# The first MLP product of one layer by Strassen's seven products, on an fp32 kernel of two transformer layers

## The chip, the cores and the metric

The kernel runs on one core of a Trainium2 chip. The metric is device time in microseconds (us): the median of the runs of one program. A profile is one more execution of the same program, in which every instruction is recorded.

The engines are TensorE (PE in the rows; its weight loads are a row of their own, PEld), VectorE (DVE), ScalarE (ACT), GpSimd (POOL) and SyncE (SP, which starts most transfers). Each engine works through its own instructions in program order; an instruction whose inputs are not there, or whose output buffer is still in use, holds up all that stand behind it on its engine. TensorE writes into PSUM, eight banks per core, the other engines into SBUF.

## The reference, cut to what matters

```python
def squared_relu_mlp(h, w1, w2):
    return jnp.square(jax.nn.relu(h @ w1)) @ w2

for layer in range(2):
    mod_x = silu(c) @ ada_w[layer] + ada_b[layer]      # six vectors of 1024; mod_c likewise for the context
    hx = modulate(rmsnorm(x, norm1_g[layer]), sh1, sc1)
    mx, mc = hybrid_mixer(hx, hc, w_in[layer], ...)    # retention and gated linear attention, 4 heads each
    x = x + g1 * (mx @ w_out[layer])
    hx = modulate(rmsnorm(x, norm2_g[layer]), sh2, sc2)
    x = x + g2 * squared_relu_mlp(hx, w_mlp1[layer], w_mlp2[layer])
    # the same for the 256 context tokens, in the first layer only
return rmsnorm(x, final_g)
```

There are 512 latent and 256 context tokens, 1024 features, 4096 hidden features, all in fp32. What is changed is `h @ w1` of the first layer, 768 tokens x 1024 x 4096.

## The kernel before, in words

Activations lie with features on the partitions: eight tiles of 128 features x 768 tokens. A product in fp32 is made from three products of a shorter type, float32r: each operand is split into a high part (a cast, `hi`, on ScalarE) and a low part (the rest, `lo`, a subtraction), and `mm3` (L437 to L439) issues high by high, high by low and low by high. A k tile (128 of the summed features) of an output tile thus takes three matmuls over 512 tokens and three over 256.

Weights come as slabs of 128 x 1024 (512 KB). `Slab.split` makes the two parts, the cast on ScalarE (L244) and the subtraction on VectorE (L245), into a ring of `NSPL` = 6 slots. `run` goes through a list of items in order; before and behind each item `advance` emits the splits of the slabs that come next, as far as the ring allows: a slab may take a slot when the last item that uses that slot's slab has been emitted.

The MLP of layer 1 (`l == 0`) runs in 8 blocks of 512 hidden features. Four `m1` items per block make the hidden features: each ends in a chain (`m1_chain`, L1207 to L1212) of ReLU and square on ScalarE, the exact square on GpSimd and the low part `hidl` on VectorE. `m2` items then multiply them by the second weight, and `residual` (L535, VectorE) adds each finished PSUM bank into `x`. Seven PSUM banks rotate under all these products (an eighth is kept for small ones), so that an eighth product must wait until the first one's bank has been read. The `m2` items of block u stand between the `m1` items of block u + 1. A chain's next step is emitted when the next item ticks (`Chains.tick`), so the order on every engine is the order in which the items emit.

In the same stretch `ada_sums` works out layer 2's six modulation vectors: 96 VectorE instructions of 128 x 1024 multiply `ada_w` by the condition and add (L340, L342), one pair per small `ada` item.

Of the kernel before, what the change touches and what calls it, by code (L numbers as in the profile page):

```python
# [9 lines left out]
F32 = mybir.dt.float32  # L10
# [6 lines left out]
P = 128  # L17
D = 1024
# [11 lines left out]
UFF = 512  # L30
UT = UFF // P
NU = FF // UFF
WCOL = 1024
NSLOT = 36
NSPL = 6
NRAW = 4
AHEAD = 4


class Item:  # L40
    """A piece of the program: emits instructions; may need weight slabs; a stage runs one block after its deps."""
# [54 lines left out]
class Act:  # L96
    """A moving operand in two float32r parts, made by chains for token ranges."""
# [10 lines left out]
# one block of projections and the attention stages that run behind it, per line; at most NSLOT tiles live  # L108
# [30 lines left out]
def build(ctx: ExitStack, tc, a):  # L139
# [44 lines left out]
    # ---- constants and inputs  # L184
# [32 lines left out]
    # silu(c) of both vectors, as 32 stationary columns (30 of them zero) per k tile  # L217
# [100 lines left out]
    # the second layer's: weighted sums over the k tiles on the vector engine, one product to add the partitions  # L318
# [5 lines left out]
    def ada_sums(l):  # L324
        acc = tp.tile([P, 2, WCOL], F32, tag="rtab", name=f"adaacc_{l}")
        todo = [(u, kk) for u in range(6) for kk in range(KK)]

        def load(i):
            u, kk = todo[i]
            w = wraw.tile([P, WCOL], F32, tag="raw", name=f"adaw_{l}_{u}_{kk}")  # L330
            nc.sync.dma_start(w, a["ada_w"][l, kk * P : (kk + 1) * P, u * WCOL : (u + 1) * WCOL])
            return w

        nxt = load(0)
        for i, (u, kk) in enumerate(todo):
            w, nxt = nxt, load(i + 1) if i + 1 < len(todo) else None
            for v in range(2):
                c = cs[:, kk, v : v + 1]
                if kk == 0:
                    nc.vector.tensor_scalar(acc[:, v], w, c, None, op0=ALU.mult)  # L340
                else:
                    nc.vector.scalar_tensor_tensor(acc[:, v], w, c, acc[:, v], op0=ALU.mult, op1=ALU.add)  # L342
            yield
            if kk == KK - 1:
                pt = psa.tile([P, 512], F32, tag="psa", name=f"ada_{l}_{u}")
                for v in range(2):
                    for c in range(4):
# [1087 lines left out]
```

## Time and profile before

| what | us |
|---|---|
| runs, median (lowest, highest) | 1659.98 (1659.19, 1660.61) |
| span of the profiled execution | 1658.9 |
| TensorE busy | 1618.7 |
| VectorE busy | 946.9 |
| ScalarE busy | 629.5 |
| GpSimd busy | 201.6 |

The profiled execution's span runs from the first instruction to the last and lies 1.1 us below the median of the runs; a time worked out from the trace is carried to the runs by adding that. Busy times are sums over instructions, and overlapping ones on TensorE are counted once.

### The profile page before, as it was taken

To read this page: it belongs to the slowest core of one execution; us is meant where nothing else is said; L and a number is where in the kernel's file an instruction comes from. 1 tells how busy PE (TensorE), PEld (TensorE's weight loads), DVE (VectorE), ACT (ScalarE), POOL (GpSimd) and SP (SyncE) were. 2 spreads that over 40 slices of the span, in tenths; PEclk is the share of its full clock that TensorE was granted. 3 is DMA by queue.
4 is the path that set the end of the run, shared out by engine and by line. 5 is a ranking of instruction groups with operands and counts; after the bars stand their busy time and mean duration, and the time that the engine had idled before them with its cause. 6 is when DMAs were issued, how large, how long until landed. Compare 5 with 4: busy or idle time off the path is not lost. (4 is left out here: it accounts for less than half of the span.)

```text
span 1658.9 us, 22890 instructions
## 1 busy us (share of the span) xinstructions
PE 1618.7 (98%) x9236; PEld 1384.2 (83%) x9236; DVE 946.9 (57%) x1491; ACT 629.5 (38%) x1083; POOL 201.6 (12%) x215
## 2 busy tenths in 40 slices
PE   5999999999999999999999999999999899999997
PEld 3778888888998888888888887888889888888887
DVE  5676664554755555555556476588466633443445
ACT  5535424562532222222212246363464532222232
POOL 3200021110111010110101121001110211010010
PEclk9999999999999999999999999999999999999999
DMA  9533433122323333333333222121123323223321
GB/s 323 175 127 126 137 108 102 39 88 90 103 89 127 115 127 109 120 102 116 126 115 127 95 88 66 51 77 52 51 89 128 103 89 102 91 100 102 102 64 51
DMA packets 57610, 173.80 MB, mean 105 GB/s; under 512 B 6208, under 2 KB 17792, under 8 KB 57504
## 3 DMA queue, kind: packets, MB, share of 16 engines
q1 hardware_dynamic: 55232, 164.85, 30.2%
q0 software_dynamic: 2272, 7.50, 1.2%
q8 instruction: 72, 1.18, 0.3%
q14 instruction: 34, 0.28, 0.0%
HBM read 168.13 MB, written 4.19 MB: 104 GB/s over the span
## 5 line engine op out<-in xcount | busy, mean ns | idle before, releaser
L437 PE MATMUL pm<-yh,hi_m 128*128 128x512 f32 (+1 forms) x800 | 279.6, 349 | 0.0
L437 PE MATMUL pm<-hidh,hi_m 128*128 128x512 f32 (+1 forms) x800 | 279.1, 349 | 0.0
L438 PE MATMUL pm<-yl,hi_m 128*128 128x512 f32 (+1 forms) x800 | 278.6, 348 | 0.0
L438 PE MATMUL pm<-hidl,hi_m 128*128 128x512 f32 (+1 forms) x800 | 278.4, 348 | 0.0
L439 PE MATMUL pm<-yh,lo_m 128*128 128x512 f32 (+1 forms) x800 | 278.2, 348 | 0.0
L439 PE MATMUL pm<-hidh,lo_m 128*128 128x512 f32 (+1 forms) x800 | 277.2, 347 | 0.0
L1208 ACT ACTIVATE relu<-pm 128x512 f32<-128x512 f32 (+1 forms) x100 | 51.1, 511 | 497.6 <-PE pm L439 493.9
L1212 DVE TENSOR_TENSOR hidl<-relu,hidh 128x512 fp32r<-128x512 f32 (+1 forms) x100 | 60.5, 607 | 296.0 <-POOL relu L1210 296.0
L1210 POOL TENSOR_TENSOR relu<-relu 128x512 f32<-128x512 f32 (+1 forms) x100 | 89.2, 893 | 760.3 <-ACT hidh L1209 760.2
L535 DVE SCALAR_TENSOR_TENSOR x<-pm,mod,x 128x512 f32<-128x512 f32 (+1 forms) x200 | 117.6, 640 | 106.6 <-PE pm L439 106.6
L437 PEld LDWEIGHTS pm<-yh,hi_m 128*128 128x128 f32 x800 | 152.6, 191 | 20.2 <-issue 1.2
L437 PEld LDWEIGHTS pm<-hidh,hi_m 128*128 128x128 f32 x800 | 151.5, 189 | 21.3 <-issue 1.1
L438 PEld LDWEIGHTS pm<-yl,hi_m 128*128 128x128 f32 x800 | 152.5, 191 | 18.8
L439 PEld LDWEIGHTS pm<-yh,lo_m 128*128 128x128 f32 x800 | 152.4, 191 | 19.0
L439 PEld LDWEIGHTS pm<-hidh,lo_m 128*128 128x128 f32 x800 | 151.1, 189 | 19.6
L438 PEld LDWEIGHTS pm<-hidl,hi_m 128*128 128x128 f32 x800 | 151.4, 189 | 18.9 <-issue 0.2
L245 DVE TENSOR_TENSOR lo_m<-raw_m,hi_m 128x1024 fp32r<-128x1024 f32 x126 | 154.0, 1222 | 10.6 <-ACT hi_m L244 10.6
L244 ACT CAST hi_m<-raw_m 128x1024 fp32r<-128x1024 f32 x128 | 129.6, 1040 | 51.6 <-DMA raw_m<-in_w_mlp 31.0
L342 DVE SCALAR_TENSOR_TENSOR adaacc<-adaw,cs,adaacc 128x1024 f32<-128x1024 f32 x84 | 103.9, 1278 | 0.0
L245 DVE TENSOR_TENSOR lo_wi<-raw_wi,hi_wi 128x1024 fp32r<-128x1024 f32 x49 | 60.6, 1249 | 29.8 <-ACT hi_wi L244 29.8
L437 PE MATMUL pwo<-yh,hi_wo 128*128 128x256 f32 (+1 forms) x224 | 70.9, 316 | 0.1
L438 PE MATMUL pwo<-yl,hi_wo 128*128 128x256 f32 (+1 forms) x224 | 70.3, 314 | 0.3 <-DVE yl L1056 0.3
(304 smaller groups left out, 2951.5 us busy)
## 6 DMA issues: line engine op xcount, KB each, us to landing
raw_m<-in_w_mlp SPq DMA_DIRECT2D x128, 512.0 KB, 3.5
adaw<-in_ada_w SPq DMA_DIRECT2D x80, 512.0 KB, 3.9
raw_wi<-in_w_in SPq DMA_DIRECT2D x58, 512.0 KB, 4.3
adaw<-in_ada_w SPq DMA_DIRECT2D x32, 256.0 KB, 6.3
raw_wo<-in_w_out SPq DMA_DIRECT2D x16, 512.0 KB, 3.4
x<-in_xT POOLq DMA_DIRECT2D x8, 384.0 KB, 7.8
x<-in_xT SPq DMA_DIRECT2D x8, 256.0 KB, 4.9
raw_wob<-in_w_out SPq DMA_DIRECT2D x4, 512.0 KB, 4.3
```

Source lines behind the costliest of these rows:

```text
L244: nc.scalar.copy(self.hi, self.raw)
L245: self.engine.tensor_sub(self.lo, self.raw, f32(self.hi))
L342: nc.vector.scalar_tensor_tensor(acc[:, v], w, c, acc[:, v], op0=ALU.mult, op1=ALU.add)
L437: nc.tensor.matmul(out, wh, xh, start=first, stop=False)
L438: nc.tensor.matmul(out, wh, xl, start=False, stop=False)
L439: nc.tensor.matmul(out, wl, xh, start=False, stop=last)
L535: nc.vector.scalar_tensor_tensor(xs[kk][:, t0:t1], pt[:, 0 : t1 - t0], mod[l][:, v, gate + kk : gate + kk + 1], xs[kk][:, t0:t1], op0=ALU. ...
L1208: nc.scalar.activation(r, pt[:, 0 : t1 - t0], AF.Relu)
L1210: nc.gpsimd.tensor_mul(r, r, r)
L1212: nc.vector.tensor_sub(a_.lo[:, t0:t1], r, f32(a_.hi[:, t0:t1]))
```

## The change: what it does

**The first MLP product of layer 1.** Layer 1's MLP now has 16 blocks u of 256 hidden features (`UTS` = (2, 4)); layer 2 keeps 512. Blocks 0 and 1 are computed as before. Blocks 2 to 15 take the Strassen-Winograd form: the weight of the block is cut in 2 x 2 (two output tiles by two halves of the 1024 features), the activations in 2 x 2 (two halves of the features by two halves of 384 tokens), and seven products of 384 tokens over 4 k tiles take the place of eight. That is 7 x 4 x 3 = 84 matmuls of 384 columns per block where 2 x 8 x 3 = 48 of 512 and 48 of 256 stood.

**Sums around it.** Four sums of weight quarters per block (`Pair.parts`: `s3`, `s1` in place in `a21`, `s2`, `s4`) are made on GpSimd, their casts on ScalarE and their low parts on VectorE. The sums of activations (`right_front`, `right_back`) are made once, during blocks 0 and 1. VectorE adds the products up (`u2`, `u3`, `c22`, `c21`, `c12`).

**What moves beside it.** The ring of split slabs has 5 slots (a `Pair` takes three and a small buffer of its own, `wsum`). Each `m2` item now covers two output tiles (`batch=2`), and layer 1 has twice as many, since a block has half the k tiles. `ada_sums` takes 64 steps of 768 columns, and the sums of the second condition are made as a product on ScalarE and an addition on GpSimd. The rotary and decay tables leave their own pool for the `work` slots (36 to 46 of them).

```diff
-NSPL = 6
+UTS = (2, 4)
+NSPL = 5
...
+    class Pair:
+        size, raws, held = 3, 2, 0
...
+        def split(self):
+            self.chain = ch.start(self.parts())
+
+        def parts(self):
+            h = WCOL // 2
+            (a11, a12), (a21, a22) = [(t[:, 0:h], t[:, h:WCOL]) for t in self.raw]
+            s2, s3, s4 = [temp(f"s{i}_{self.name}") for i in (2, 3, 4)]
+            nc.gpsimd.tensor_sub(s3, a11, a21)
+            nc.gpsimd.tensor_add(a21, a21, a22)
...
+            split(self.raw[0], hi[0], lo[0])
+            yield
+            nc.gpsimd.tensor_sub(s2, a21, a11)
+            nc.gpsimd.tensor_sub(s4, a12, s2)
+            two()
+            split(self.raw[1], hi[1], lo[1])
+            self.held = 0
+            yield
+            two()
+            split(s3, hi[2][:, 0:h], lo[2][:, 0:h])
+            split(s2, hi[2][:, h:WCOL], lo[2][:, h:WCOL])
+            yield
...
+            split(s4, hi[3], lo[3])
...
     def ada_sums(l):
...
-            for v in range(2):
-                c = cs[:, kk, v : v + 1]
...
-                    nc.vector.scalar_tensor_tensor(acc[:, v], w, c, acc[:, v], op0=ALU.mult, op1=ALU.add)
...
+                nc.vector.scalar_tensor_tensor(acc[0], w, c0, acc[0], op0=ALU.mult, op1=ALU.add)
+                nc.scalar.mul(w, w, c1)
+                nc.gpsimd.tensor_add(acc[1], acc[1], w)
...
+        def right_front(k):
...
+            for w, kk in ((t, k), (u, k + KH)):
+                nc.gpsimd.tensor_add(w, f32(norm2.out[kk].hi[:, 0:NT]), f32(norm2.out[kk].lo[:, 0:NT]))
+            yield
+            nc.gpsimd.tensor_sub(t[:, 0:H], t[:, H:NT], t[:, 0:H])
+            nc.vector.tensor_sub(t[:, H:NT], u[:, H:NT], t[:, H:NT])
+            yield
+            nc.gpsimd.tensor_sub(u[:, H:NT], u[:, H:NT], t[:, 0:H])
+            nc.gpsimd.tensor_sub(u[:, 0:H], u[:, 0:H], u[:, H:NT])
...
+        def product(pair, nm, x, pt, first=True):
+            ch.finish(pair.chain)
+            hi, lo, c0 = pair.part[nm]
+            for k in range(KH):
+                w = slice(c0 + k * P, c0 + k * P + P)
+                xh, xl = right[x, k]
+                for i, (wt, xt) in enumerate(((hi, xh), (hi, xl), (lo, xh))):
+                    nc.tensor.matmul(
+                        pt[:, 0:H], wt[:, w], xt, start=first and k == 0 and i == 0, stop=k == KH - 1 and i == 2,
+                        skip_group_check=True,
+                    )
+            ch.tick()
...
+            def p1():
+                product(pair, "a11", "b11", open_(1))
...
+            def p6():
+                product(pair, "s2", "t2", open_(2))
+                out(2, "u2", st["p1"])
+
+            def p7():
+                product(pair, "s3", "t3", open_(3))
+                out(3, "u3", st["u2"])
+
+            def p5():
+                product(pair, "s1", "t1", open_(4))
+                tail(out(4, "c22", st["u3"]), 1, H)
+
+            def p2():
+                product(pair, "a12", "b21", p[1], False)
...
+            def p4():
+                product(pair, "a22", "t4", p[3], False)
+                tail(out(3, "c21", st["u2"]), 1, 0)
+
+            def p3():
+                product(pair, "s4", "b22", p[4], False)
+                tail(out(4, "c12", st["u2"]), 0, H)
...
+            for u in range(2):
+                for i, q in enumerate(quarters):
+                    m2_item(u, [q], ada=False, batch=2)
...
+            strassen_items(2)
+            for u in range(2, NU - 1):
+                strassen_items(u + 1)
+                for q in quarters:
+                    m2_item(u, [q], batch=2)
```

**VectorE where an `m2` begins.** Before, around the first `m2` items of block 3 of 512 features (`lo_m1`, `lo_m2` are splits of slabs, `x0_0` the first output tile's residual, `adaacc` the modulation sums):

```order
L342 SCALAR_TENSOR_TENSOR adaacc_1_4292<-adaw_1_2_5_5841,cs_139,adaacc_1_4292 128x1024 x2
L245 TENSOR_TENSOR lo_m2_0_3_2_5920<-raw_m2_0_3_2_5845,hi_m2_0_3_2_5919 128x1024
L535 SCALAR_TENSOR_TENSOR x0_0_3342<-pm2_0_3_0_0_5923,mod0_149,x0_0_3342 128x512
L535 SCALAR_TENSOR_TENSOR x0_0_3342<-pm2_0_3_0_512_5924,mod0_149,x0_0_3342 128x256
L535 SCALAR_TENSOR_TENSOR x0_1_3344<-pm2_0_3_1_0_5925,mod0_149,x0_1_3344 128x512
L535 SCALAR_TENSOR_TENSOR x0_1_3344<-pm2_0_3_1_512_5926,mod0_149,x0_1_3344 128x256
L342 SCALAR_TENSOR_TENSOR adaacc_1_4292<-adaw_1_2_6_5913,cs_139,adaacc_1_4292 128x1024 x2
L245 TENSOR_TENSOR lo_m2_0_3_3_5986<-raw_m2_0_3_3_5917,hi_m2_0_3_3_5985 128x1024
L1212 TENSOR_TENSOR hidl_0_16_5990<-relu_0_16_0_6016,hidh_0_16_5989 128x512
L1212 TENSOR_TENSOR hidl_0_16_5990<-relu_0_16_512_6046,hidh_0_16_5989 128x256
L342 SCALAR_TENSOR_TENSOR adaacc_1_4292<-adaw_1_2_7_5979,cs_139,adaacc_1_4292 128x1024 x2
L245 TENSOR_TENSOR lo_m1_0_18_6058<-raw_m1_0_18_5983,hi_m1_0_18_6057 128x1024
```

Here one split stands between a step and the next residual.

VectorE now, around the beginning of `m2` of block 6 of 256 (whose hidden features are 12 and 13), behind the Strassen products of block 7 (hidden 14 and 15); the name `m1s_0_8` is the pair of block 8, rows with L1424 are `out`, L515 is `split`, L616 is `residual`:

```order
L1424 TENSOR_TENSOR c21_0_7_6210<-pst3_0_7_6138,u2_0_7_6131 128x384
L397 SCALAR_TENSOR_TENSOR adaacc_1_0_4626<-adaw_1_3_6_6176,cs_139,adaacc_1_0_4626 128x768
L1406 TENSOR_TENSOR hidl_0_15_6169<-c21_0_7_6210,hidh_0_15_6168 128x384
L1424 TENSOR_TENSOR c12_0_7_6233<-pst4_0_7_6153,u2_0_7_6131 128x384
L515 TENSOR_TENSOR lo0_m1s_0_8_6246<-raw_m1s_0_8_0_6090,hi0_m1s_0_8_6245 128x1024
L1406 TENSOR_TENSOR hidl_0_14_6194<-c12_0_7_6233,hidh_0_14_6193 128x384
L515 TENSOR_TENSOR lo1_m1s_0_8_6258<-raw_m1s_0_8_1_6092,hi1_m1s_0_8_6257 128x1024
L515 TENSOR_TENSOR lo2_m1s_0_8_6265<-s3_m1s_0_8_6241,hi2_m1s_0_8_6264 128x512
L515 TENSOR_TENSOR lo2_m1s_0_8_6265<-s2_m1s_0_8_6240,hi2_m1s_0_8_6264 128x512
L515 TENSOR_TENSOR lo3_m1s_0_8_6274<-s4_m1s_0_8_6242,hi3_m1s_0_8_6273 128x512
L616 SCALAR_TENSOR_TENSOR x0_0_3347<-pm2_0_6_0_0_6249,mod0_149,x0_0_3347 128x512
L616 SCALAR_TENSOR_TENSOR x0_0_3347<-pm2_0_6_0_512_6250,mod0_149,x0_0_3347 128x256
```

All five low parts of the pair of block 8 now stand ahead of the first residual of `m2` of block 6. The same order stands at the beginning of `m2` of blocks 2 to 13, each time with the pair two blocks on.

**GpSimd at the same place**, where before only the squares of the hidden features stood (L1404 is the square, L274 to L286 the sums of the pair):

```order
L1404 TENSOR_TENSOR c11_0_7_6191<-c11_0_7_6191 128x384
L1404 TENSOR_TENSOR c21_0_7_6210<-c21_0_7_6210 128x384
L399 TENSOR_TENSOR adaacc_1_1_4627<-adaacc_1_1_4627,adaw_1_3_6_6176 128x768
L1404 TENSOR_TENSOR c12_0_7_6233<-c12_0_7_6233 128x384
L274 TENSOR_TENSOR s3_m1s_0_8_6241<-raw_m1s_0_8_0_6090,raw_m1s_0_8_1_6092 128x512
L275 TENSOR_TENSOR raw_m1s_0_8_1_6092<-raw_m1s_0_8_1_6092 128x512
L285 TENSOR_TENSOR s2_m1s_0_8_6240<-raw_m1s_0_8_1_6092,raw_m1s_0_8_0_6090 128x512
L286 TENSOR_TENSOR s4_m1s_0_8_6242<-raw_m1s_0_8_0_6090,s2_m1s_0_8_6240 128x512
L399 TENSOR_TENSOR adaacc_1_1_4627<-adaacc_1_1_4627,adaw_1_3_7_6218 128x768
```

The four sums of a pair stand behind the squares of `c21` and `c12`, the last two results of the products.

**ScalarE where layer 1's projections turn from `vg` to `vr`** (the last of the copies of `vg` banks and what stands behind it), before:

```order
L763 COPY vg_0_3_706<-ps_vg0_5_962 128x128
L244 CAST hi_wi0_11_993<-raw_wi0_11_697 128x1024
L244 CAST hi_wi0_12_999<-raw_wi0_12_991 128x1024
L825 ACTIVATE gest_0_1_1011<-gst_0_1_919 128x18
L830 ACTIVATE gl_0_1_832<-gt_0_1_831,c_sgn_99 128x768
```

and now:

```order
L848 COPY vg_0_3_705<-ps_vg0_5_961 128x128
L248 CAST hi_wi0_10_992<-raw_wi0_10_696 128x1024
L248 CAST hi_wi0_11_998<-raw_wi0_11_990 128x1024
L248 CAST hi_wi0_12_1004<-raw_wi0_12_996 128x1024
L910 ACTIVATE gest_0_1_1016<-gst_0_1_918 128x18
```

Slab 10, which `vr` begins with, is cast behind the copies now, where its cast stood ahead of all of them before; layer 2 has the same order.

## Rows read from the trace of the kernel before

**Rows 1.** The page: busy time of each engine.

```profile
PE 1618.7 (98%) x9236; PEld 1384.2 (83%) x9236; DVE 946.9 (57%) x1491; ACT 629.5 (38%) x1083; POOL 201.6 (12%) x215
```

**Rows 2.** Windows: a stretch in layer 1's MLP (busy, granted clock).

```profile
core 0: us, PE busy (x) PEld busy (x) DVE busy (x) ACT busy (x) POOL busy (x), PEclk, DMA share, GB/s
470.00:970.00 500.00, 500.00 (x2909) 436.62 (x2908) 279.46 (x362) 120.06 (x185) 51.30 (x65) 1.00 0.36 116
```

**Rows 3.** Waits of TensorE, whole span: first and last of eleven rows.

```profile
PE ada L382 <- DMA adaw<-in_ada_w: 11.8, 1, 11.8
...
PE ps_d L452 <- DVE hl_n L521: 0.3, 1, 0.3
```

**Rows 4.** Timeline of TensorE in layer 1's MLP: start, duration, instruction.

```profile
599.12 0.39 PE L438 MATMUL pm<-yl,hi_m 128*128 128x512 f32 x1
...
601.61 0.28 PE L437 MATMUL pm<-yh,hi_m 128*128 128x256 f32 x1
...
602.45 0.28 PE L438 MATMUL pm<-yl,hi_m 128*128 128x256 f32 x1
```

**Rows 5.** Groups of VectorE by shape: count, busy us, mean ns, idle before.

```profile
L245 DVE TENSOR_TENSOR lo_m<-raw_m,hi_m 128x1024 fp32r<-128x1024 f32 x126 | 154.0, 1222 | 10.6 <-ACT hi_m L244 10.6
L342 DVE SCALAR_TENSOR_TENSOR adaacc<-adaw,cs,adaacc 128x1024 f32<-128x1024 f32 x84 | 103.9, 1278 | 0.0
L535 DVE SCALAR_TENSOR_TENSOR x<-pm,mod,x 128x512 f32<-128x512 f32 x120 | 87.6, 749 | 102.5 <-PE pm L439 102.5
...
L1212 DVE TENSOR_TENSOR hidl<-relu,hidh 128x512 fp32r<-128x512 f32 x60 | 42.5, 708 | 248.6 <-POOL relu L1210 248.6
L535 DVE SCALAR_TENSOR_TENSOR x<-pm,mod,x 128x256 f32<-128x256 f32 x80 | 37.0, 475 | 4.0 <-PE pm L439 4.0
...
L1212 DVE TENSOR_TENSOR hidl<-relu,hidh 128x256 fp32r<-128x256 f32 x40 | 18.1, 456 | 47.4 <-POOL relu L1210 47.4
```

**Rows 6.** Groups of ScalarE, shapes apart.

```profile
L244 ACT CAST hi_m<-raw_m 128x1024 fp32r<-128x1024 f32 x128 | 129.6, 1040 | 51.6 <-DMA raw_m<-in_w_mlp 31.0 <-PE pm L438 20.4 <-DVE hidl L1212 0.2
...
L1209 ACT ACTIVATE hidh<-relu 128x512 fp32r<-128x512 f32 x60 | 37.9, 632 | 1.9
L1208 ACT ACTIVATE relu<-pm 128x512 f32<-128x512 f32 x60 | 35.9, 598 | 442.8 <-PE pm L439 442.8
...
L1208 ACT ACTIVATE relu<-pm 128x256 f32<-128x256 f32 x40 | 15.3, 382 | 54.7 <-PE pm L439 51.0 <-DVE hidl L1212 3.7
```

**Rows 7.** Groups of GpSimd, shapes apart.

```profile
L1210 POOL TENSOR_TENSOR relu<-relu 128x512 f32<-128x512 f32 x60 | 63.6, 1060 | 699.9 <-ACT hidh L1209 699.8
L1210 POOL TENSOR_TENSOR relu<-relu 128x256 f32<-128x256 f32 x40 | 25.6, 642 | 60.4 <-ACT hidh L1209 60.4
...
L946 POOL TENSOR_TENSOR rq<-rq,rw_q 128x512 f32<-128x512 f32 x8 | 10.3, 1286 | 137.3 <-DVE rw_q L945 136.9
...
L983 POOL TENSOR_TENSOR rq<-rq,rtab 128x768 f32<-128x768 f32 x4 | 8.0, 1996 | 1.2 <-PE prs L966 1.0
```

**Rows 8.** Timeline of GpSimd and VectorE around 422 us, before layer 1's MLP.

```profile
422.09 1.29 POOL L510 TENSOR_TENSOR xn_n<-x,ssum_n 128x512 f32<-128x512 f32 x1 [3.31 <-DVE yl L521]
...
422.43 2.04 DVE L245 TENSOR_TENSOR lo_wob<-raw_wob,hi_wob 128x1024 fp32r<-128x1024 f32 x1 [0.47 <-ACT hi_wob L244]
```

**Rows 9.** Timeline of TensorE at its longest wait inside layer 2.

```profile
1297.16 0.80 PE L490 MATMUL st_n<-ssum_n,ones_d 128*128 128x256 f32 x1 [4.43 <-DVE ssum_n L473]
```

**Rows 10.** Windows behind that wait; columns as in Rows 2.

```profile
1297.00:1300.00 3.00, 2.84 (x11) 2.66 (x12) 2.62 (x4) 0.89 (x2) 1.16 (x2) 0.50 0.67 195
1300.00:1304.00 4.00, 4.00 (x26) 4.00 (x26) 3.57 (x8) 2.65 (x6) 1.03 (x2) 0.66 0.32 118
```

**Rows 11.** Timeline of ScalarE and VectorE where layer 2 turns from vg to vr.

```profile
1041.24 0.77 ACT L763 COPY vg<-ps_vg 128x128 f32<-128x128 f32 x4 [4.67 <-PE ps_vg L439]
...
1042.99 2.36 DVE L245 TENSOR_TENSOR lo_wi<-raw_wi,hi_wi 128x1024 fp32r<-128x1024 f32 x2 [1.72 <-ACT hi_wi L244]
```

**Rows 12.** Timeline of VectorE where layer 1 ends: layer 2's norm.

```profile
976.85 1.42 DVE L521 SCALAR_TENSOR_TENSOR hl_n<-xn_n,mod,hh_n 128x512 fp32r<-128x512 f32 x2
```

More of the change, by code (lines that the diff above doesn't have):

```diff
@@ L324, in ada_sums @@
     def ada_sums(l):
-        acc = tp.tile([P, 2, WCOL], F32, tag="rtab", name=f"adaacc_{l}")
-        todo = [(u, kk) for u in range(6) for kk in range(KK)]
+        acc = [work(f"adaacc_{l}_{v}") for v in range(2)]
+        todo = [(u, kk) for u in range(6 * D // T) for kk in range(KK)]
         def load(i):
@@ L1212, in m1_chain, with hidden @@
             nc.vector.tensor_sub(a_.lo[:, t0:t1], r, f32(a_.hi[:, t0:t1]))
+        def hidden(u, m):
+            if (u, m) not in hid:
+                j = u * UT + m
+                hid[u, m] = Act(work(f"hidh_{l}_{j}", F32R), work(f"hidl_{l}_{j}", F32R))
+            return hid[u, m]
         def m1_part(u, m, groups):
@@ L1217, in fn @@
             def fn():
-                if (u, m) not in hid:
-                    hid[u, m] = Act(work(f"hidh_{l}_{j}", F32R), work(f"hidl_{l}_{j}", F32R))
+                h = hidden(u, m)
                 for t0, t1 in groups:
@@ L1222, in fn, with m2_part @@
                     project(pt, m1[j], 0, norm2.out, t0, t1)
[L1223 to L1224 removed]
+                    c = ch.start(m1_chain(h, pt, f"{l}_{j}_{t0}", t0, t1))
+                    h.made.append((t0, t1, c))
             return fn
[L1228 removed]
+        def m2_part(u, jps, groups, last, batch=4):
             def fn():
@@ L1252, in m2_part @@
             return fn
+        H = NT // 2
+        KH = KK // 2
+        right = {}
+        def right_front(k):
+            t, u = [work(f"sum_{l}_{k}_{i}")[:, 0:NT] for i in range(2)]
+            right["sum", k] = t, u
+            for w, kk in ((t, k), (u, k + KH)):
[6 more added lines that the diff above has]
+            nc.gpsimd.tensor_sub(u[:, 0:H], u[:, 0:H], u[:, H:NT])
@@ new lines, in hidden_chain, with strassen_items, tail, open_ @@
+        def hidden_chain(c, a_, t0, relu):
+            if relu:
+                yield
+            hh, hl = a_.hi[:, t0 : t0 + H], a_.lo[:, t0 : t0 + H]
+            if relu:
+                nc.scalar.activation(c, c, AF.Relu)
+            nc.scalar.activation(hh, c, AF.Square)
+            nc.gpsimd.tensor_mul(c, c, c)
+            yield
+            nc.vector.tensor_sub(hl, c, f32(hh))
+        def strassen_items(u):
+            pair = pairs[u]
+            st, p = {}, {}
+            nm = f"{l}_{u}"
+            def tail(c, m, t0, relu=True):
+                h = hidden(u, m)
+                h.made.append((t0, t0 + H, ch.start(hidden_chain(c, h, t0, relu))))
+            def open_(i):
+                p[i] = bank(f"pst{i}_{nm}")
+                return p[i]
+            def out(i, nm_, other):
+                c = st[nm_] = temp(f"{nm_}_{nm}")[:, 0:H]
+                nc.vector.tensor_add(c, p[i][:, 0:H], other)
+                return c
+            def p1():
+                product(pair, "a11", "b11", open_(1))
+                st["p1"] = temp(f"p1_{nm}")[:, 0:H]
+                nc.scalar.copy(st["p1"], p[1][:, 0:H])
+            def p6():
[9 more added lines that the diff above has]
+                product(pair, "a12", "b21", p[1], False)
+                c = temp(f"c11_{nm}")[:, 0:H]
+                nc.scalar.activation(c, p[1][:, 0:H], AF.Relu)
+                tail(c, 0, 0, False)
+            def p4():
[4 more added lines that the diff above has]
+                tail(out(4, "c12", st["u2"]), 0, H)
+            for i, fn in enumerate((p1, p6, p7, p5, p2, p4, p3)):
+                plan.append(Item(f"st{i}.{u}", fn, [pair]))
+                if i % 2:
+                    plan.append(Item("ada", mlp_ada))
```

197 lines of the change are left out of this document (146 added, 51 removed).

## The prediction

> **What bounds the kernel now.** I read the page first: TensorE is busy for 1618.7 of 1658.9 us [rows 1]. An engine that full leaves little to win by filling gaps, and the list of its waits confirms it: eleven kinds, the longest a single wait of 11.8 us at the start for weights, the last 0.3 [rows 3]. The windows then show the stretch that is changed: from 470 to 970 us, nearly all of layer 1's MLP, TensorE is busy for 500.00 of 500 us at a granted clock of 1.00, while VectorE does 279.46, ScalarE 120.06 and GpSimd 51.30 [rows 2]. There TensorE alone sets the time, so matmul columns taken away are time won, but only as long as the other engines still hand over everything in time. Whether they do is read from their queues.
>
> **What the Strassen form takes away.** The timeline gives the spacing: eleven matmuls of 512 columns start within 601.61 − 599.12 = 2.49 us, 0.2264 each, and seven of 256 within 602.45 − 601.61 = 0.84, 0.120 each [rows 4]. A block of 256 features took 48 pairs, 48 × 0.3464 = 16.63 us. It now takes 84 matmuls of 384, by interpolation 0.173 each: 14.55. Fourteen blocks win 14 × 2.08 = **−29.1 us**. The second product has as many matmuls as before.
>
> The Trainium skill (TensorE: Matmul & The Clock Gate, section "Back-to-back issue gap") gives N/2.4 + 2.5 ns for an isolated matmul; an estimate by it is 15.60 − 13.65 = 1.95 us per block, 27.3 in all. The same section gives 131 ns for 512 columns in a sustained stream, which the 226 of these rows contradict.
>
> **What the order does at each block boundary.** An `m2` step of two groups is 6 matmul pairs, 6 × 0.3464 = 2.08 us, and a block's `m2` uses two banks per output tile. With seven banks in rotation the eighth bank (the second of output tile 3) is the first one's, so TensorE passes 3 × 2.08 + 0.68 = 6.92 us from the start of `m2` before it needs the first residual to be done. Before, one split stood ahead of a residual (first piece of order). Now the order on VectorE puts all five low parts of the pair two blocks on ahead of it, and they wait for the pair's sums on GpSimd, which stand behind the squares of the block's last two results, which wait for the last product.
>
> I time that chain from the end of the last product (P3), which is where `m2` begins. Sizes of 384 are midway between the 512 and 256 rows: an addition out of PSUM like `x` 0.61, `hidl` 0.58 [rows 5], ReLU 0.49, its square by the same difference 0.53 [rows 6], the exact square 0.85 [rows 7]. `c21`, one product (2.08 us) earlier, is out at −1.4, has its ScalarE squares at −0.3, GpSimd's at 0.6, and its `hidl` at 1.2. `c12` stands behind that `hidl`: out 1.8, ReLU 2.3, square 2.8. From 2.8 on GpSimd has the square (0.85) and four sums of 512, 1.06 to 1.29 each [rows 7], together 5.1 to 6.0; VectorE has low parts of 1.22, 1.22 and three of 0.71, and a `hidl` of 0.58 [rows 5], together 5.15. Do these overlap? The timeline has a case: GpSimd's `xn_n` runs from 422.09, and the `lo_wob` that starts at 422.43 takes 2.04 us instead of 1.22 [rows 5, 8]. That is 0.82 more, most of the 0.95 for which the two lie over each other (422.43 to 423.38). So one of the two stands still while the other reads. I count them one after the other: 2.8 + 5.1 + 5.15 + 0.75 (first residual) = 13.8 us with the short sums, 14.7 with the long ones. TensorE wanted it at 6.92: a stall of 6.9 to 7.8.
>
> The Trainium skill (SBUF — State Buffer, section "Who interferes with whom") calls the port shared by VectorE and GpSimd an exclusive lock, taken by a VectorE instruction with two SBUF inputs. The row at 422.43 agrees; no run here shows yet what it does to this chain.
>
> If they did overlap, the chain goes through GpSimd and ScalarE: square 3.7, `s3` 4.7, `s1` 5.8, `s2` 6.8, `s4` 7.9, its cast 0.6, low part 0.7, residual 0.75, 10.0 in all, and a stall of 3.1. That is the lower bound. The upper bound adds an `ada` addition on GpSimd, 768 columns, up to 2.0 us [rows 7], which in the rows of the order stands between the two squares: about 9.5. Nearest to the traced case is the serial sum; I take 7.0. It stands at `m2` of blocks 2 to 13, 12 times: **+84 us** (37 to 114).
>
> **The clock after a stall.** In layer 2 TensorE waits for 4.43 us for `ssum_n`, and then the granted clock is 0.50 for 3 us and 0.66 for 4, against 1.00 in the MLP [rows 2, 9, 10]. That loses 3 × 0.50 + 4 × 0.34 = 2.9 us; I take 2.8, and none for the lower bound. 12 × 2.8 = **+34 us** (0 to 35).
>
> **Two places that happen once.** The products of block 3 follow those of block 2 with no `m2` between them, and their pair can be split only when block 2's has been used. P6 needs the low part of `s2`: 2.8 + 5.1 + 1.22 + 0.58 + 1.22 + 1.42 = 12.3 us behind P3 of block 2, less the 2.1 of P1, a stall of 10.2, with the clock **+13** (bounds 5 and 15). The pair of block 2 is made while the activation sums run on GpSimd (four chains of two additions of 768 columns and three of 384, about 7 us each by [rows 7]), with `m2` of block 1's residuals behind it; I estimate 6 and the clock, **+8.8** (0 to 14).
>
> **Smaller terms.** With five slots, slab 10 is cast behind the `vg` copies (last piece of order). In layer 2 before, the last copies begin at 1041.24, and the first low part behind them is done at 1042.99 + 1.18 = 1044.17 [rows 11]; it was slab 11's and is now slab 10's, which TensorE wants first, some 2.9 us earlier. Other products can lie between; 1.7 in each layer, **+3.4** (0 to 5.8). At the end of layer 1 only half as much `m2` work (a block of 256: 4.3 us for the context's part, it was 8.6) covers layer 2's norm, whose first low parts come at 976.85 [rows 12]: **+3** (0 to 4.3). At nothing I cost the casts of the pairs on ScalarE (ScalarE is at 24% [rows 2]; without that cover they are in the chain already), the transfers (the same bytes of weights), and the doubled residuals, which the second product hides: 8 × (0.75 + 0.475) = 9.8 us of VectorE in 16.6 [rows 5].
>
> **The modulation sums.** They lie on all engines for the first ten blocks: 7 steps per block. Of 72 calls 64 are steps and 56 have an addition on GpSimd, so a block has 6.2 steps and 5.4 additions. GpSimd then has 4 squares, 4 sums and these: 4 × 0.85 + 4 × 1.06 + 5.4 × 1.9 = 17.9 us (1.9 being 1.5 times the 1.29 of 512). VectorE's instructions with two SBUF inputs are seven low parts (2 × 1.22 and 3 × 0.71 of the pair, 2 × 1.22 of the second weight) 7.0, four `hidl` 2.3 and 6.2 sums of 768 at 0.96, three quarters of 1.278 [rows 5]: 15.3. If they exclude each other that is 33.2 us in a block of 14.55 + 16.63 = 31.2. It is in a rival.
>
> **Sum**, on the span: −29.1 + 84 + 34 + 13 + 8.8 + 3.4 + 3 = +117, so 1658.9 + 117 = 1776, and 1777 with the 1.1 us that the runs lie above the span. A difference under 0.2% (3.3 us) couldn't be told from none.
>
> **The rivals.**
> - *The chain overlaps or the clock does not fall.* Stalls of 3.1 and a clock price: 12 × 5.9 = 71 in place of 118, 1730; with no clock price as well, 12 × 3.1 = 37 and the single places at half, some 1685. For it: each rests on one place of the trace, and the stall at 1297.16 is followed by a stretch with 2.84 of 3 us busy, so other small gaps lie in it [rows 10]. Against it: the 2.04 us and the windows at 0.50. 0.22.
> - *The common reads bind.* In ten blocks 33.2 us and up, with hand-overs, 2 to 4 us each above the forecast: 1800 to 1815, more if stalls and it add. For it: the sum above. Against it: a stall of 7 us lengthens the block, and so gives these engines the time they lack. 0.12.
> - *The stalls are hidden: faster.* If the first residual lands within 6.92 us of the start of `m2`, or no more than 2.08 × 14 / 12 = 2.4 us late without a price for the clock, the gain wins: with all hidden, 1660 − 29 + 3 to 6 = 1635. It decides at the point where the pair's sums do not wait for the squares. For it: VectorE and GpSimd have idle time on the average. Against it: both take their instructions in order. 0.05. Exactly cancelling, 0.02.
>
> Main case, 1735 to 1800: 0.59. With the lower part of the first rival the range is **1690 to 1815**; left out are the faster cases, the ends of the first and the tail of the second, about 0.2. Faster 0.05, same 0.02, slower 0.93.
>
> **What would show it.** In the trace after: TensorE idle at the second bank of output tile 3 in each `m2` of blocks 2 to 13, ended by VectorE's `x`, some 7 us; ahead of it on VectorE low parts of the pair with idle time that GpSimd's sums end; a granted clock well below 1.00 behind each stall; 84 matmuls in 14.6 us where nothing stalls; a wait in P1 and P6 of block 3. If `x` is on time there, or the clock stays at 1.00 after the stalls, the prediction falls at that step.

## The result, and the profile after

The changed kernel takes 1834.67 us (median of 4 runs, 1830.91 to 1837.89), the kernel before 1660.3 beside it: a ratio of 1.1051, with an interval of 1.1032 to 1.1070. It is slower by 174 us. The forecast was 1777, slower by 117, and the range ended at 1815.

The page of the profiled execution (span 1835.4 us), with the busy times that answer to [rows 1] and the slices of granted clock:

```profile
PE 1642.2 (89%) x9072; PEld 1412.9 (77%) x9072; DVE 1123.7 (61%) x1717; ACT 731.0 (40%) x1219; POOL 436.2 (24%) x347
...
PEclk8999999999797888889988889999999999999999
```

TensorE has fewer matmuls and is busy 89% of a longer span; before it was 98%. A slice is 45.9 us; from the 11th to the 24th, 459 to 1101 us, which is the MLP of layer 1, most slices of the clock are at 7 or 8 tenths. What TensorE waited for in the whole span (total, times, longest), the rows that answer to [rows 3]:

```profile
PE pm L518 <- DVE x L616: 101.0, 13, 13.9
PE ada L407 <- POOL adaacc L399: 16.0, 8, 2.3
PE pst L1390 <- ACT hi_m1s L514: 15.1, 2, 7.8
...
PE adat L323 <- ACT adarow L318: 8.4, 3, 7.4
...
PE pm L519 <- DVE hidl L1300: 3.6, 1, 3.6
```

The wait for the residual `x` that the prediction named leads, 13 times. One of the 13 is not at a boundary: it is the longest, 13.9 us, at `m2` of block 0. Another is a wait of 1 us at the last block. The boundary of block 10 is not among them: a small transpose stood next in TensorE's queue there, and its wait, 7.4 us, is the main part of the row of `adat`. So the 12 boundaries cost 101.0 − 13.9 − 1 + 7.4 = 93.5 us, 7.8 each.

One boundary, `m2` of block 7, which begins at 808.1 us. The timeline of GpSimd (start, duration, instruction; `c` are results of the products, `s_m1s` and `raw_m1s` the sums of the pair):

```profile
805.56 1.83 POOL L399 TENSOR_TENSOR adaacc<-adaacc,adaw 128x768 f32<-128x768 f32 x1 [0.48 <-ACT adaw L398]
807.35 0.82 POOL L1404 TENSOR_TENSOR c<-c 128x384 f32<-128x384 f32 x1
810.43 0.83 POOL L1404 TENSOR_TENSOR c<-c 128x384 f32<-128x384 f32 x1 [2.25 <-ACT hidh L1403]
811.32 2.24 POOL L399 TENSOR_TENSOR adaacc<-adaacc,adaw 128x768 f32<-128x768 f32 x1
813.52 0.83 POOL L1404 TENSOR_TENSOR c<-c 128x384 f32<-128x384 f32 x1
814.30 1.28 POOL L274 TENSOR_TENSOR s_m1s<-raw_m1s,raw_m1s 128x512 f32<-128x512 f32 x1
815.66 2.13 POOL L275 TENSOR_TENSOR raw_m1s<-raw_m1s 128x512 f32<-128x512 f32 x1
817.87 1.46 POOL L285 TENSOR_TENSOR s_m1s<-raw_m1s,raw_m1s 128x512 f32<-128x512 f32 x1
819.41 2.13 POOL L286 TENSOR_TENSOR s_m1s<-raw_m1s,s_m1s 128x512 f32<-128x512 f32 x1
```

VectorE at the same time:

```profile
808.21 0.56 DVE L1406 TENSOR_TENSOR hidl<-c,hidh 128x384 fp32r<-128x384 f32 x1 [2.54 <-POOL c L1404]
808.68 0.55 DVE L1424 TENSOR_TENSOR c<-pst,u 128x384 f32<-128x384 f32 x1
...
811.29 0.56 DVE L1406 TENSOR_TENSOR hidl<-c,hidh 128x384 fp32r<-128x384 f32 x1 [1.13 <-POOL c L1404]
811.76 0.55 DVE L1424 TENSOR_TENSOR c<-pst,u 128x384 f32<-128x384 f32 x1
814.41 2.26 DVE L515 TENSOR_TENSOR lo_m1s<-raw_m1s,hi_m1s 128x1024 fp32r<-128x1024 f32 x1 [2.10 <-ACT hi_m1s L514]
816.59 1.61 DVE L1406 TENSOR_TENSOR hidl<-c,hidh 128x384 fp32r<-128x384 f32 x1
818.90 1.52 DVE L515 TENSOR_TENSOR lo_m1s<-raw_m1s,hi_m1s 128x1024 fp32r<-128x1024 f32 x1 [0.70 <-ACT hi_m1s L514]
820.34 2.95 DVE L515 TENSOR_TENSOR lo_m1s<-s_m1s,hi_m1s 128x512 fp32r<-128x512 f32 x3
823.21 2.18 DVE L616 SCALAR_TENSOR_TENSOR x<-pm,mod,x 128x512 f32<-128x512 f32 x4
```

And TensorE's wait:

```profile
824.01 0.58 PE L518 MATMUL pm<-hidh,hi_m 128*128 128x256 f32 x1 [8.79 <-DVE x L616]
```

The chain is the one that was written down: squares of the last results, four sums on GpSimd, five low parts on VectorE, then the first residual at 823.21, and TensorE goes on at 824.01. From `c12` (811.76) to the residual's start are 11.5 us; the working had 11.9 (it starts at 1.2 there, and the residual at 13.05). What is later than in the working is `c12` itself: 3.7 us after the start of `m2` instead of 1.2. An `adaacc` addition on GpSimd (805.56) holds up the square of 807.35, whose `hidl` (808.21) stands on VectorE ahead of `c21`, and `c12` comes behind `c21`'s `hidl`; the second addition (811.32) ends just when the next square has its input. In e2 below, which leaves out GpSimd's additions alone, `c12` starts 1.95 us after `m2` at the same boundary. The durations also show that GpSimd and VectorE exclude each other: the sum at 815.66 takes 2.13 us where the one at 814.30 takes 1.28, the low part at 814.41 takes 2.26 where [rows 5] have 1.22. The Trainium skill (SBUF — State Buffer, section "Who interferes with whom") describes such a lock for VectorE instructions with two SBUF inputs, and these rows bear it out.

The windows of the wait and behind it (busy time and count of PE, PEld, DVE, ACT, POOL, then the granted clock):

```profile
814.00:824.00 10.00, 1.21 (x7) 0.73 (x5) 8.89 (x8) 3.16 (x5) 7.30 (x5) 0.66 0.28 85
824.00:827.00 3.00, 2.99 (x10) 2.71 (x11) 3.00 (x6) 0.65 (x1) 0.00 (x0) 0.50 0.49 199
827.00:831.00 4.00, 4.00 (x23) 3.42 (x23) 4.00 (x5) 1.23 (x2) 1.86 (x1) 0.95 0.18 35
```

Behind the wait the clock is at 0.50 for 3 us, the level of 1.2 GHz, and at 0.95 over the next 4, against the 0.66 of [rows 10]. Other boundaries have the same 3 us at 0.50 and differ in the second stretch; behind the waits that end at 595.71 (8.31 us) and 1046.59 (6.70 us) it is:

```profile
598.70:602.70 4.00, 4.00 (x24) 3.47 (x23) 4.00 (x5) 1.23 (x2) 1.86 (x1) 1.00 0.18 37
...
1049.60:1053.60 4.00, 4.00 (x15) 3.32 (x15) 2.55 (x5) 0.78 (x1) 0.00 (x0) 0.62 0.23 69
```

Over the whole execution the starts of matmuls that follow one another without a gap of 0.3 us are 36.1 us later than their widths ask at full clock; in the kernel before that sum is −4.1. So the clock costs some 40 us.

Two further places. At `m2` of block 0 (VectorE, then TensorE):

```profile
497.52 0.56 DVE L1360 TENSOR_TENSOR sum<-sum,sum 128x384 f32<-128x384 f32 x1 [2.64 <-POOL sum L1359]
498.00 2.19 DVE L616 SCALAR_TENSOR_TENSOR x<-pm,mod,x 128x512 f32<-128x512 f32 x4
...
498.80 0.58 PE L518 MATMUL pm<-hidh,hi_m 128*128 128x256 f32 x1 [13.88 <-DVE x L616]
```

The activation sums (`right_front`) run on GpSimd from 465 to 500 us, one of their subtractions is VectorE's (L1360), and it stands ahead of `m2` of block 0's first residual: TensorE waits 13.88 us. At the second pair (SyncE, GpSimd, ScalarE, TensorE):

```profile
546.44 10.23 SPq L241 DMA_DIRECT2D raw_m<-in_w_mlp  x2
...
555.05 1.26 POOL L286 TENSOR_TENSOR s_m1s<-raw_m1s,s_m1s 128x512 f32<-128x512 f32 x1
...
560.01 1.04 ACT L248 CAST hi_m<-raw_m 128x1024 fp32r<-128x1024 f32 x1 [9.35 <-DMA raw_m<-in_w_mlp]
560.96 1.04 ACT L514 CAST hi_m1s<-raw_m1s 128x1024 fp32r<-128x1024 f32 x1
...
563.10 0.69 PE L1390 MATMUL pst<-t4h,hi_m1s 128*128 128x384 f32 x1 [7.85 <-ACT hi_m1s L514]
```

Here ScalarE waits 9.35 us for a slab of the second weight. SyncE's row has that transfer and one before it, and is done with them at 556.67, just after the pair's sum of 555.05 has ended at 556.31. By these times the transfer had to wait until that sum had read the buffer which it fills. Behind ScalarE's wait its queue has the cast of the pair at 560.96. TensorE waits 7.85 us for it, on top of 7.24 a product earlier.

And the product of the modulation sums, one of eight:

```profile
605.96 1.07 PE L407 MATMUL ada<-adaacc,onehot 128*32 128x256 f32 x6 [2.33 <-POOL adaacc L399]
```

It waits for GpSimd's addition of the second condition; eight such waits are 16.0 us in the list of waits, and by the starts of the matmuls around them some 6 us more go there.

### The profile page after: what moved, and what is told of

It reads as the page before. It is cut to its first block, busy times and chain, and to the rows that moved or that the text cites. A ratio compares the mean times of both kernels' runs of the same rounds, so it can differ in the third digit from the quotient of the medians.

```text
span 1835.4 us, 23277 instructions
## 1 busy us (share of the span) xinstructions
PE 1642.2 (89%) x9072; PEld 1412.9 (77%) x9072; DVE 1123.7 (61%) x1717; ACT 731.0 (40%) x1219; POOL 436.2 (24%) x347
## 5 line engine op out<-in xcount | busy, mean ns | idle before, releaser
L518 PE MATMUL pm<-hidh,hi_m 128*128 128x512 f32 (+1 forms) x800 | 295.6, 369 | 101.0 <-DVE x L616 101.0
L616 DVE SCALAR_TENSOR_TENSOR x<-pm,mod,x 128x512 f32<-128x512 f32 (+1 forms) x328 | 188.0, 624 | 55.3 <-PE pm L520 55.1
L399 POOL TENSOR_TENSOR adaacc<-adaacc,adaw 128x768 f32<-128x768 f32 x56 | 106.2, 1897 | 187.7 <-ACT adaw L398 174.9
L518 PE MATMUL pm<-yh,hi_m 128*128 128x512 f32 (+1 forms) x352 | 128.2, 364 | 0.0
L519 PE MATMUL pm<-yl,hi_m 128*128 128x512 f32 (+1 forms) x352 | 127.8, 363 | 0.0
L520 PE MATMUL pm<-yh,lo_m 128*128 128x512 f32 (+1 forms) x352 | 127.6, 362 | 0.0
L398 ACT ACTIVATE adaw<-adaw,cs 128x768 f32<-128x768 f32 x56 | 52.4, 935 | 132.3 <-DVE adaacc L397 100.2
L1404 POOL TENSOR_TENSOR c<-c 128x384 f32<-128x384 f32 x56 | 50.9, 909 | 174.9 <-ACT hidh L1403 166.7
L1390 PE MATMUL pst<-yh,hi_m1s 128*128 128x384 f32 x224 | 77.4, 346 | 7.2 <-ACT hi_m1s L514 7.2
L1390 PE MATMUL pst<-yh,lo_m1s 128*128 128x384 f32 x224 | 76.7, 343 | 1.3 <-DVE lo_m1s L515 1.3
L1390 PE MATMUL pst<-yl,hi_m1s 128*128 128x384 f32 x224 | 76.6, 342 | 0.0
```

The costliest lines, as they stand in the source:

```text
L398: nc.scalar.mul(w, w, c1)
L399: nc.gpsimd.tensor_add(acc[1], acc[1], w)
L518: nc.tensor.matmul(out, wh, xh, start=first, stop=False)
L519: nc.tensor.matmul(out, wh, xl, start=False, stop=False)
L520: nc.tensor.matmul(out, wl, xh, start=False, stop=last)
L616: nc.vector.scalar_tensor_tensor(xs[kk][:, t0:t1], pt[:, 0 : t1 - t0], mod[l][:, v, gate + kk : gate + kk + 1], xs[kk][:, t0:t1], op0=ALU. ...
```

## Experiments

The first three theories are: **queue** (the place of the low parts in VectorE's queue makes the stalls), **shared reads** (GpSimd's and VectorE's work together is more than a block holds), and **frame** (blocks of 256, five slots and moved tables cost by themselves). All times stand beside runs of the kernel before on the same chip, 1659.8 to 1660.2 us.

**e1: the low parts behind the residuals.** The pair's four sums are issued together, and one step of its casts and low parts behind each quarter of `m2`.

```diff
-            self.chain = ch.start(self.parts())
+            self.chain = Chain(self.parts())
+            self.chain.step()
+            pair_now[0] = self.chain
...
+            nc.gpsimd.tensor_sub(s2, a21, a11)
+            nc.gpsimd.tensor_sub(s4, a12, s2)
...
+            yield
             split(self.raw[0], hi[0], lo[0])
...
+                if pair_now[0]:
+                    pair_now[0].step()
```

> The changed kernel, with the pair's parts in another order: the four sums are issued together on GpSimd, and one step of casts and low parts follows behind each quarter of m2, so that the first residual stands ahead of all five low parts. Same work. Queue theory (the stall is the place in VectorE's queue): the 12 waits of TensorE for x at m2 of blocks 2 to 13, 95 us in the profile after, fall to under 10, and of the 40 us that the lowered clock costs some 28 go with them: 1835 - 90 - 28 = about 1715. Rival (VectorE and GpSimd together have more work in a block than TensorE, because they share reads): the wait moves to another place and the time stays above 1790.

Measured: 1790.66 us (ratio 1.0787, 1.0771 to 1.0803), 44 us less than the changed kernel where 120 were expected. The waits of TensorE:

```profile
PE pm L520 <- DVE x L618: 40.8, 19, 13.7
PE ada L408 <- DVE adaacc L398: 21.0, 8, 4.2
PE ada L408 <- POOL adaacc L400: 17.5, 8, 2.7
PE pst L1395 <- ACT hi_m1s L516: 16.2, 1, 16.2
```

The waits for `x` fall from 101.0 to 40.8 us, 13.7 of them still at block 0, but 38 us are now lost on the modulation sums' products, and 16 at the second pair. Far from the queue theory's number, and at the rival's bound of 1790, within the runs' spread (1789.16 to 1791.95): the stalls of the queue are gone, and behind them stands another wait, which the sums make.

**e2: without GpSimd's additions of the modulation sums.**

```diff
-                nc.gpsimd.tensor_add(acc[1], acc[1], w)
```

> The changed kernel without GpSimd's additions of the second condition's modulation sums (56 additions of 128 x 768 are left out, so the context's modulation in layer 2 is that of the last k tile alone). Queue theory: these additions only delay the squares, some 1 us at each boundary that they reach, and the modulation products, 8 waits of 2 us with 2 us around each: the 12 waits for x fall from 8.0 to 6.9 us each, and the time to about 1800. Rival (shared reads bind): with 106 us of GpSimd's work gone the waits for x collapse, and the time falls below 1740.

Measured: 1794.35 us (1.0810, 1.0793 to 1.0826), 40 us less. The waits that stay:

```profile
PE pm L517 <- DVE x L615: 90.9, 13, 14.9
...
PE adat L323 <- ACT adarow L318: 7.6, 3, 6.4
```

Reckoned as in the profile after, the twelve boundaries take 90.9 − 14.9 − 1 + 6.4 = 81.4 us, 6.8 each, where 6.9 were expected: in the changed kernel's own order the queue makes them, as its theory had it.

**e3: the frame without Strassen.** All 16 blocks compute their first product as before.

```diff
-            for u in range(2, NU - 1):
-                strassen_items(u + 1)
+            for u in range(1, NU - 1):
+                for m in range(UT):
+                    m1_item(u + 1, m)
+                plan.append(Item("ada", mlp_ada))
                 for q in quarters:
                     m2_item(u, [q], batch=2)
```

> The changed kernel without the Strassen form: all 16 blocks of 256 features compute their first product as before, everything else as changed (blocks, five slots, modulation sums on three engines, table loads). Queue theory: no pairs, no stalls for x; what is left are the smaller terms, vg to vr 2 to 3 us, the norm 3, waits of the modulation products up to 16: 1664 to 1685. Rival (the doubled residuals and the modulation sums on GpSimd are a cost of their own): above 1700.

Measured: 1730.45 us (1.0429, 1.0411 to 1.0446). This is the rival's case: without a single pair, 70 us of the 174 are there. The groups of VectorE and GpSimd from 560 to 860 us show the low parts of ordinary slabs at 1768 ns, and the addition beside them:

```profile
L249 DVE TENSOR_TENSOR lo_m<-raw_m,hi_m 128x1024 fp32r<-128x1024 f32 x30 | 53.0, 1768 | 59.7 <-ACT hi_m L248 59.7
...
L399 POOL TENSOR_TENSOR adaacc<-adaacc,adaw 128x768 f32<-128x768 f32 x40 | 78.8, 1970 | 137.5 <-ACT adaw L398 131.8 <-DVE x L616 5.3
```

**e4: late sums of activations, and three standard blocks.** `right_front` stands behind the quarters of `m2` of block 0, `right_back` behind those of block 1, and block 2 is standard, so that every Strassen block has an `m2` ahead of it.

```diff
+            for i, q in enumerate(quarters):
+                m2_item(0, [q], ada=False, batch=2)
+                plan.append(Item(f"front{i}", lambda k=i: fronts.append(ch.start(right_front(k)))))
+            for m in range(UT):
+                m1_item(2, m, ada=False)
+            for i, q in enumerate(quarters):
+                m2_item(1, [q], ada=False, batch=2)
+                plan.append(Item(f"back{i}", lambda k=i: back(k)))
```

> The changed kernel with a third standard block, and with the sums of activations behind the quarters of m2 of block 0 and their parts behind those of block 1 (in the changed kernel they stand ahead of m2 of block 0); the products of the first Strassen block no longer follow one another without an m2 between. Theory: gone are the stall of 13.9 us and 3.6 at m2 of block 0, 18.6 us at the second pair, one boundary of 8 and their share of the clock, some 10; 2 us come back for the third standard block: 1835 - 52 = about 1783. Rival: GpSimd's 28 us of sums hold up m2 of block 1 instead, and the time falls by less than 20.

Measured: 1803.83 us (1.0863, 1.0847 to 1.0879), 31 us less: between the theory's 52 and the rival's 20.

**f1: e1 and e2 together.**

> The order of e1 and the omission of e2 in one kernel (GpSimd's 56 additions of the second condition's sums are left out, so the context's modulation in layer 2 is that of the last k tile alone). Apart, the two won 44 and 40 us. If they remove different waits they add up: about 1750. If the additions are what fills the time that the order frees (the reads that GpSimd and VectorE share bind once the queue is right), more goes than the sum: below 1725, with the waits for x in blocks 4 to 12 under 10 us together.

Measured: 1728.37 us (1.0410, 1.0395 to 1.0426), 106 us less than the changed kernel, where 44 and 40 would add to 84. So the two meet: part of what the order frees, the additions had taken. It stopped 3 us above the bound that was set for that, and the waits for `x` from block 4 on add up to some 12 us, more than the 10 named.

**f2: the frame with both modulation sums on VectorE.**

```diff
-                nc.scalar.mul(w, w, c1)
-                nc.gpsimd.tensor_add(acc[1], acc[1], w)
+                nc.vector.scalar_tensor_tensor(acc[1], w, c1, acc[1], op0=ALU.mult, op1=ALU.add)
```

> The frame without Strassen (e3, 1730 us) with both conditions' modulation sums on VectorE, two instructions of 128 x 768 per step, as the kernel before had them with 1024. Nothing is left out. If the 70 us that the frame costs come from the sums' additions on GpSimd and what they hold up, it falls to 1665 to 1680. If they come from the doubled residuals and the blocks of 256, it stays above 1700; VectorE's work of about 29 us in a block of 33.3 would then be too much with its waits.

Measured: 1692.18 us (1.0194, 1.0177 to 1.0211), 38 us less than e3 and 12 above the upper end of what was expected. The same group of low parts as in e3's view now:

```profile
L249 DVE TENSOR_TENSOR lo_m<-raw_m,hi_m 128x1024 fp32r<-128x1024 f32 x33 | 40.2, 1217 | 2.9 <-ACT hi_m L248 2.9
```

1217 ns where e3 has 1768: GpSimd's additions were what held them up. The frame's cost is not gone with them: 32 us are left.

**f3: Strassen with e1, e4 and both sums on VectorE.**

> The Strassen kernel with three edits: one step of the pair behind each quarter of m2 (e1), three standard blocks and late sums of activations (e4), and both conditions' modulation sums on VectorE, spread thinner (six calls a block, none behind P7, P5 or P3, from block 0 on, and one call more before each sum's product). Nothing is left out. If the order and the shared reads are the whole of the loss, TensorE's stream is what is left, 1660 - 13 x 2.08 + 6 for the smaller terms: 1635 to 1665, on either side of the kernel before. If VectorE, with some 31 us of work in a block of 31.2, binds: 1680 to 1720.

Measured: 1761.12 us (1.0606, 1.0591 to 1.0622), a miss for both. VectorE is busy for 228 of 300 us there, so it is not full; the waits that lead on TensorE are for its residuals (41.2 us) and its additions of products (25.7).

**g1, g2, g3: without the sums.** The loads stay, only the first of eight k tiles is multiplied: Strassen with e1 and e4 (g1), the kernel before (g2, where both sums are VectorE's one line), the frame (g3). Without their readers the loads' buffers also come free sooner, by the program, so these runs take away the sums' work and their hold on the buffers together.

```diff
-                nc.vector.scalar_tensor_tensor(acc[0], w, c0, acc[0], op0=ALU.mult, op1=ALU.add)
-                nc.scalar.mul(w, w, c1)
-                nc.gpsimd.tensor_add(acc[1], acc[1], w)
+                pass
```

> The Strassen kernel with the order of e1 and e4 and without layer 2's modulation sums: their loads stay, but only the first of eight k tiles is multiplied and none is added, on any engine (layer 2's modulation is that of one k tile). If the pair's order, the late sums of activations and the modulation sums are the whole of the loss, TensorE's stream is left, 13 blocks 2.08 us shorter each, with the small terms that the frame also has (the norm behind layer 1, vg to vr): 1640 to 1660. If Strassen's own additions and low parts bind VectorE (22 us of work in 31.2, in bursts): above 1690.

> The kernel before without the same sums (loads stay, 84 instructions of VectorE are left out). There TensorE waits for nothing in the stretch in which they run: 1655 to 1661, no change. If it falls by over 5 us, the sums cost something before too.

> The frame without Strassen (e3) without the same sums. What of its 70 us is left is the price of the blocks of 256, the five slots and the moved tables: 1662 to 1675. g1 against this kernel is the Strassen form alone, with the engines free: 13 x 2.08 = 27 us less if nothing else stands in its way; no less than this kernel if the pair's work eats the gain.

Measured: g1 1658.15 us (0.9987, 0.9977 to 0.9996), g2 1659.89 (0.9999, 0.9990 to 1.0008), g3 1673.05 (1.0075, 1.0060 to 1.0090). All three lie where they were expected if the sums are what costs, g1 near its upper end. The sums cost the kernel before nothing. Without them the frame costs 13.1 us, and Strassen in the better order is 14.9 us faster than the frame, about half of the 27 that its columns are worth. The window of g1 from 560 to 860 us:

```profile
560.00:860.00 300.00, 300.00 (x1766) 274.50 (x1765) 203.54 (x330) 102.10 (x160) 85.66 (x72) 1.00 0.45 143
```

TensorE is busy for all of it at full clock; what g1 lacks of 27 us lies outside, mostly at the first blocks: by the starts of its matmuls it waits 10.0 us between 400 and 600 us where g3 waits 2.5, and the clock falls behind that.

**g4: e1 and e4 with the sums as changed,** but with their steps behind P1 and P6 and the quarters of `m2`, where they stood behind P6, P5 and P4.

> The Strassen kernel with the order of e1 and e4 and the modulation sums on VectorE, ScalarE and GpSimd as changed, but with none of their steps between the last products of a block (they stand behind P1 and P6 and the quarters of m2). Nothing is left out. If e1 (44 us) and e4 (31 us) add up: 1760. If the additions on GpSimd fill what they free: 1775 to 1790. It is faster than the kernel before only if the sums hide altogether, which f3 speaks against.

Measured: 1773.59 us (1.0682, 1.0666 to 1.0698), 61 us less than the changed kernel where 75 would be the sum; it lies just under the 1775 to 1790 named for additions that fill what the order frees. Its main waits:

```profile
PE pst L1395 <- DVE u L1429: 33.3, 8, 4.9
PE pm L520 <- DVE x L618: 25.2, 20, 2.4
```

They are for VectorE's additions of products and its residuals. Against g1, which has the same order of pairs without the sums, the sums cost 115 us. Without them the better order of e1 and e4 is worth 129 us (h1 below, 1787.0, against g1's 1658.2), with them 61. VectorE itself waits here for the loads of `ada_w`, 17 times, with all that stands behind them in its queue:

```profile
DVE adaacc L398 <- DMA adaw<-in_ada_w: 39.6, 17, 3.3
```

**h1: the changed kernel's own order without the sums.**

> The changed kernel in its own order, without layer 2's modulation sums (as g1: loads stay, the first k tile is multiplied and nothing is added). It tells the price of the order from that of the sums. By the chain of the prediction, 12 waits for x of 6.9 us each (83) with a clock price of 2.8 (34), the waits at m2 of block 0 (17) and at the second pair (12 to 18) stand on top of g1's 1658, which has one Strassen block fewer: 1790 to 1810, the waits at all twelve boundaries equal. If the order alone costs less and the sums make the waits long: under 1760, waits of 3 to 4 us.

Measured: 1787.01 us (1.0763, 1.0745 to 1.0781), 3 under the lower end of the first case. Its waits, and three of its boundaries:

```profile
PE pm L516 <- DVE x L614: 89.0, 13, 15.0
...
PE adat L323 <- ACT adarow L318: 7.3, 3, 6.1
PE pst L1388 <- DVE lo_m1s L513: 5.0, 2, 3.7
PE pst L1388 <- ACT hi_m1s L512: 4.8, 2, 4.1
```

```profile
587.34 0.58 PE L516 MATMUL pm<-hidh,hi_m 128*128 128x256 f32 x1 [6.74 <-DVE x L614]
...
711.50 0.58 PE L516 MATMUL pm<-hidh,hi_m 128*128 128x256 f32 x1 [5.36 <-DVE x L614]
...
1040.71 0.58 PE L516 MATMUL pm<-hidh,hi_m 128*128 128x256 f32 x1 [6.74 <-DVE x L614]
```

With the boundary of the `adat` row, the twelve take 89.0 − 15.0 − 1 + 6.1 = 79.1 us, 6.6 each; most single rows show 6.74 us, in early blocks and late ones alike, the shortest 5.36.

## Why the prediction was right or wrong

**Columns: right.** 84 matmuls of 384 take 14.6 us where nothing stalls (793.5 to 808.1 us for block 8's), as worked out from the spacing. The working counted eleven kinds of wait before, the last of 0.3 us [rows 3]; the whole list has thirteen, the last two of 0.2, which changes nothing.

**The boundary stall: right in place, chain and size.** The working gave 6.9 and took 7.0. In h1, without the sums, the mean wait is 6.6 and most are 6.74; with the sums but without GpSimd's additions (e2) it is 6.8; in the profile after it is 7.8. So 1.0 of the 1.2 more comes with GpSimd's `adaacc` additions, which delay the squares; the upper bound had 2.0 for that. The two boundaries behind the sums' end (from 1010 us on) wait 6.7 and 6.8.

**The clock: right in sum.** 34 and 5.6 at the two single places, some 40 measured. The price came from one place, and single stalls differ from it (0.62 to 1.00 in the second stretch, where it had 0.66), so that the sum agrees so closely is partly luck.

**The two single places: wrong in size, one in cause.** Block 0: 6 taken, 13.9 and 3.6 (the `hidl` row of the waits) measured. It isn't the pair of block 2 with block 1's residuals, but VectorE's own subtraction of the activation sums ahead of block 0's, so the working looked one block too late. The activation sums took 35 us on GpSimd where it had four times 7, and without the modulation sums the wait is no less (15.0 in h1). The second pair: 10.2 taken, 7.24 + 1.28 + 7.85 + 1.07 = 17.4 measured in four waits. A transfer for a buffer that the pair itself held stood in the chain; the transfers had been priced at nothing, "the same bytes". Without the sums it is 5.0 + 4.8 = 9.8 (h1), near the working.

**The modulation sums: the step that failed.** They were left out of the sum and put in a rival of 0.12, with 33.2 us of common reads in a block of 31.2, "2 to 4 us each". That text takes the stalls and the common reads as alternatives, on the ground that a stall gives these engines the time they lack; that they might add is named, without a price. They add: h1 is 1787.0, 10 us above the forecast without any sums, and the sums make it 1834.7, 47.7 more. Of these the profile shows 16.0 + 6 at the products, 14 at the boundaries (93.5 against 79.1), 8 at the second pair (17.4 against 9.8), and 7 of the clock (40 against 33, reckoned the same way), together 51. In this order GpSimd's additions are most of it: e2 leaves these out alone and is 40 us faster. The products' wait for the sums had no term at all, since the kernel before has none.

**The smaller terms: right in kind.** vg to vr costs 0.68 + 1.03 us in layer 1 and 0.61 + 1.09 in layer 2 in g3, 3.4 as forecast. The frame without sums costs 13.1 instead of the 6.4 named; the rest was not taken apart. It is not at layer 2's norm alone: g3's waits for `ps_gq` are 3.7 us where they were 1.0, those of `st_n` 9.7 where they were 5.7.

**Added up,** the changed kernel's difference is −28.8 for the columns (14 × 2.06), 93.5 at the boundaries, 17.5 and 17.4 at the two single places, 22 at the products of the sums, 40 of the clock and 13.1 of the frame: 174.7, against 174.4 measured. The terms are good to a few us each, so part of that agreement is luck.

What stays open is why f3 and g4, with the good order, still lose over 100 us while no engine is full. The rows show VectorE waiting for squares on GpSimd and TensorE for VectorE, with the two excluding each other. But g1 has as long a wait for squares (90.8 us, against 87.7 in g4 and 89.2 in f3), so this wait alone is not it. VectorE's wait for the loads of `ada_w` (39.6 us in g4, 13.9 in f3) is another candidate. Which hand-over binds was not separated by a run. No version here beats the kernel before: g1 is 0.13% faster, less than the 0.2% that the prediction set for telling a difference, and it leaves the sums out.

## What to carry to other kernels

Here the columns taken from a full engine were paid for by the engines beside it. So write down, for one block, the chain that the new form adds between the last product and the first thing that TensorE needs back, and count banks against it. Work that was free under the old form (here the modulation sums, which the kernel before lost nothing by, g2) has to be priced anew under the new one, in the main sum and not as a rival. Where VectorE's instructions have two SBUF inputs, as the low parts do, their time and that of GpSimd's at the same moment are to be added, not overlapped (1768 against 1217 ns in e3 and f2); that sum alone did not give the times of f3 and g4.

## What the runs showed of the hardware that was not expected

Behind waits of 6.70, 8.31 and 8.79 us the granted clock is at 0.50 for 3 us, as it is behind the wait of 4.43 us in [rows 9, 10]. Over the next 4 us the clock is 0.62, 1.00 and 0.95 behind these three and 0.66 there, so one stall's price says little about another's. And an addition on GpSimd that has nothing to do with TensorE's stream made ordinary low parts 1768 ns long instead of 1217, in a kernel without any Strassen form (e3, f2).
